# The four smallest experts moved last, and the final normalization started beside them, in a one-core mixture-of-experts layer

## The chip, the cores and the metric

The kernel runs on one core of one Trainium2 chip. The metric is device time in microseconds (us) for one execution, the median of the runs shown. Times inside a trace are counted from the first instruction of one profiled execution.

## The reference

One decoder layer on 1024 tokens of width 1024, in float32. The first sub-layer (token mixing, a projection, a layer norm) is not touched. The second is a mixture of experts: a router picks two of 32 experts for each token; an expert is a SwiGLU block with a 1024x1024 up matrix and a 512x1024 down matrix. The end of the layer is a second layer norm:

```
m = _hier_moe(h2, ...)          # for each token: sum over its 2 experts of weight * expert(h2)
x = _layernorm(ALPHA * x + (1.0 + g2) * m, ln2_g, ln2_b)
```

## The kernel before, in words

**What is computed where.** When the router is done, a table in DRAM, `xad` (1024 rows and 128 spare ones), holds `ALPHA * x` for each token. Each expert adds its weighted result to the rows of its tokens with an indirect DMA from POOL (`scatter`, line 1415). Every scatter adds into `xad`, so each waits until the one before has landed. At the very end (lines 1543 to 1603) `xad` is read back in eight tiles of 128 rows, each is normalized and stored to `out`.

**The order of the experts.** Experts 0 to 2 stand first. The other 29 are ranked by their number of tokens, and the table `place` (lines 841 to 844) says which rank is worked on at which of the 32 places in the order. Before the change large and small ones alternate to the end: places 25, 27, 29 and 31 hold the four smallest (ranks 28 to 31), place 26 one of five experts with room for two tiles of tokens, place 28 rank 11 and place 30 rank 15. An expert with at most 32 tokens runs a four-part form (`up_parts(4)`, `down_parts(4)`: matmuls with 32 columns of weights, 128\*32 in a row), up to 48 tokens (and up to 64) a two-part form (128\*64), a larger one the whole form (128\*128).

**One step of the loop** (lines 1480 to 1505), for place e: the first half of the up matrix (`up(e, range(4), ...)`), the transposes of the hidden tile of e-1, the second half of the up matrix, `hidden` (Silu on ScalarE, product on VectorE), the transposes of the tokens of e+1 with the gather for e+3 behind them, and then `last_of(e-1)`: the down matrix of e-1, `finish(e-1)` (VectorE scales the result, POOL scatters it).

**The weight stream.** Weights come as 384 loads of 512 KB on SP's queue, in the order of the list `SEQ` (lines 763 to 766): the eight up tiles of e, then the four down tiles of e-1. There are 38 slots. `release` (line 1460) hands a used slot back and issues the next load (`eload`, line 788). When all 384 are issued, two further releases fetch the norm's two vectors (`late_v`, line 1445: ln2_g and ln2_b, each broadcast to a 128x1024 tile, `l2`). Instructions of one queue are issued in program order, so a load that has to wait holds up every load behind it on SP.

**The end.** After `last_of(31)` every engine reads one number (`most`, line 1512) and jumps over a block for very large experts (`tc.If`, line 1513), which is not taken here. Then the eight reads of `xad`, and 59 steps of normalization, whose order is the string `TORDER` (one digit for a step of that tile) and whose engines are set by `TSTAT` (moments on VectorE or ScalarE) and `TMODE` (which engine does the multiplication by ln2_g, step `both(0)`, and the addition of ln2_b, step `both(1)`). In the first thirteen steps, 0010010210121, stand the moments of tiles 0 to 2, the roots of tiles 0 and 1, and as the thirteenth the `both(0)` of tile 1 on VectorE (line 1574), the first VectorE step that needs ln2_g.

Of the kernel before, what the change touches and what calls it, by code (L numbers as in the profile page):

```python
# [23 lines left out]
P = 128  # L24
# [7 lines left out]
FIXED = 3  # L32
SPREAD = 4
BIG = (3, 5, 12, 19, 26)
CO = (1, 2)
HL = 5
WK = (6,)
# [15 lines left out]
TSTAT = "VVVSVSVS"  # L53
TMODE = "pFBpFAFF"
TORDER = "00100102101213023231320425323423564546436567545653776777575"
BACC = dict(dynamic_dma_scratch_size=7168)
COLS = [slice(0, 512), slice(512, 1024)]

# [2 lines left out]
def tile_hybrid_moe_layer(  # L61
# [31 lines left out]
    def cst(shape, dt, name):  # L93
        return const.tile(shape, dt, name=name)
# [1173 lines left out]
    def reorder():  # L1268
# [19 lines left out]
    nmax = cst([P, 1], I32, "nmax")  # L1288
    places()
    for t in (*xg[2:], *eyo, yo2, act, *wr, *wr2):  # L1290
        G.memset(t, 0.0)
# [126 lines left out]
                             compute_op=OP.add)  # L1418

    def finish(e):  # L1420
        yo = eyo[e % 2]
        by_parts(N[e], lambda: result(yo, pd(e), wr[e % 2]), lambda m: result(yo, pd(e), wr[e % 2], m))
        by_size(rows_of(e), lambda rows: scatter(yo, tokp[:, 0, e:e + 1], rows))
# [50 lines left out]
    def last_of(e):  # L1474
# [2 lines left out]
        finish(e)  # L1477
        finish_second(e)

    for e in range(NE):  # L1480
# [62 lines left out]
    l2g, l2b = l2  # L1543
# [3 lines left out]
    st8 = p4.tile([P, 8, 2, 6], F32, name="st8")  # L1547
    mv8 = p4.tile([P, 8, 2], F32, name="mv8")

    def t_ops(tt):  # L1550
        r, mode = rt[tt], TMODE[tt]
        mu, sd = mv8[:, tt, 0:1], mv8[:, tt, 1:2]

        def moments():
            for n, sl in enumerate(COLS):
                V.bn_stats(st8[:, tt, n], r[:, sl])

        def root(scale=1.0):
            S.activation(sd, sd, AF.Sqrt, bias=eps, scale=scale)

        def shift():
            if TSTAT[tt] == "V":
                V.scalar_tensor_tensor(mu, mu, -1.0, sd, op0=OP.mult, op1=OP.mult)
            else:
                V.tensor_tensor(mu, mu, sd, op=OP.mult)

        def part(q, sl, fused, e):
            v = (l2g, l2b)[q]
            if not fused:
                e.tensor_tensor(r[:, sl], r[:, sl], v[:, sl], op=(OP.mult, OP.add)[q])  # L1570
            elif q:
                V.scalar_tensor_tensor(r[:, sl], r[:, sl], sd, v[:, sl], op0=OP.mult, op1=OP.add)  # L1572
            else:
                V.scalar_tensor_tensor(r[:, sl], r[:, sl], mu, v[:, sl],  # L1574
                                       op0=OP.subtract if TSTAT[tt] == "V" else OP.add, op1=OP.mult)

        def both(q):
            e = {"p": (G, G), "F": (V, V), "A": (G, V), "B": (V, G), "X": (V, V), "q": (G, G)}[mode][q]
            for sl in COLS if tt == 7 else [slice(0, D)]:
                part(q, sl, mode == "F", e)  # L1580
                if q and tt == 7:
                    nc.sync.dma_start(out[0, tt * P:(tt + 1) * P, sl], r[:, sl])
            if q and tt < 7:
                nc.sync.dma_start(out[0, tt * P:(tt + 1) * P, :], r)

        if TSTAT[tt] == "V":
            ops = [moments, lambda: V.bn_aggr(mv8[:, tt], st8[:, tt]), root]
        else:
            ops = [lambda: S.activation(eyo[0], r, AF.Copy, accum_out=mu),
                   lambda: V.tensor_scalar(mu, mu, -1.0 / D, None, op0=OP.mult),  # L1590
                   lambda: S.activation(eyo[0], r, AF.Square, bias=mu, accum_out=sd),
                   lambda: root(1.0 / D)]
        ops.append(lambda: V.reciprocal(sd, sd))
        if mode == "q":
            ops.append(lambda: V.tensor_scalar(r, r, mu, sd, op0=OP.subtract if TSTAT[tt] == "V" else OP.add,
                                               op1=OP.mult))
        elif mode != "F":
            ops += [shift, lambda: S.activation(r, r, AF.Identity, bias=mu, scale=sd)]
        return ops + [lambda: both(0), lambda: both(1)]

    t_all = [t_ops(tt) for tt in range(8)]
    for tt in TORDER:
        run(t_all[int(tt)], 1)


_INS = ['x', 'c', 'w_ada', 'b_ada', 'w_in', 'lb_logits', 'hg_norm_w', 'sg_ln_g', 'sg_ln_b', 'sg_w', 'sg_b',
# [20 lines left out]
```

## Time and profile before

| | us |
|---|---|
| three runs | 1179.14, 1181.39, 1178.46 |
| median | 1179.14 |
| profiled execution, own time | 1183.11 |
| profiled execution, span of its trace | 1181.4 |
| TensorE busy in the span | 1042.4 (88%) |
| VectorE, ScalarE, POOL busy | 553.6, 291.6, 359.6 |

The span runs from the first to the last instruction, and the execution's own time lies 1.7 us above it. Shares over the whole span mix stages with different limits; the change concerns the last 160 us, so the rows below are from there. A row of the timeline gives the start, the time, the engine, the line, the operation with what it writes and reads, the shape, how many instructions the row merges, and in brackets how long the engine sat idle before and what released it. "SPq" is SP's queue of DMA issues: its rows show the issue, not the transfer.

### The profile page before, as it was taken

The numbers are of one execution on the slowest core, as the hardware profiler recorded it, in microseconds if no ns is written. First come the engines' busy times: TensorE is split into PE (matmuls) and PEld (weight loads), VectorE is DVE, ScalarE is ACT, GpSimd is POOL, SyncE is SP. The second block draws the span as 40 slices with busy tenths as digits, with TensorE's granted clock in tenths as the row PEclk, the third lists the DMA queues.
The fourth block names the chain that finished last, engine by engine and source line by source line (L and its number), as shares of the span: only waits on it lengthen the run. The fifth ranks groups of instructions, "written<-read, shape, count | busy, mean of one in ns | idle before, by whom it ended". The sixth has DMA issues, their size and how long they took to land. (4 is left out here: it accounts for less than half of the span.)

```text
span 1181.4 us, 17353 instructions
## 1 busy us (share of the span) xinstructions
PE 1042.4 (88%) x5758; PEld 678.4 (57%) x5758; DVE 553.6 (47%) x1018; ACT 291.6 (25%) x440; POOL 359.6 (30%) x272
## 2 busy tenths in 40 slices
PE   4999999899999989998588899999998998799930
PEld 3778888788788767776333454445433553344400
DVE  6858975738664389999410211311221121211238
ACT  3363336642234442121200110101110110110113
POOL 2325643353121145552511211321141113211215
PEclk9899999999999998999799999999998998999975
DMA  9854454343211336316899979999999999999964
GB/s 278 241 164 146 143 178 144 124 157 130 89 54 54 143 143 220 120 72 248 303 393 383 351 254 371 363 386 390 371 379 395 393 371 372 394 398 384 378 247 187
DMA packets 121282, 304.55 MB, mean 258 GB/s; under 512 B 17840, under 2 KB 45144, under 8 KB 121132
## 3 DMA queue, kind: packets, MB, share of 16 engines
q1 hardware_dynamic: 111548, 275.53, 64.1%
q0 software_dynamic: 8368, 22.90, 7.2%
q10 hardware_dynamic: 1216, 4.21, 0.9%
q8 instruction: 83, 1.36, 0.5%
q14 instruction: 67, 0.55, 0.1%
HBM read 281.09 MB, written 22.88 MB: 257 GB/s over the span
## 5 line engine op out<-in xcount | busy, mean ns | idle before, releaser
L1395 DVE TENSOR_TENSOR act<-up,act 128x512 f32<-128x512 f32 x32 | 22.1, 692 | 311.6 <-ACT act L1394 234.1
L1416 POOL DMA_INDIRECT xad<-yo,tokp x36 | 52.8, 1466 | 228.4 <-DVE yo L1412 141.5
L1412 DVE SCALAR_TENSOR_TENSOR yo<-dn,wr,g2p 32x256 f32<-32x256 f32 (+2 forms) x94 | 52.1, 563 | 127.4 <-PE ov L1348 49.3
L1401 ACT ACTIVATE eh<-tp 128x512 f32<-128x512 f32 x36 | 21.1, 596 | 311.3 <-PE tp L1400 268.5
L1207 POOL DMA_INDIRECT KS<-h2d,tokp x32 | 30.5, 954 | 191.5 <-PE tp L1311 182.8
L622 PE MATMUL acc<-whi,hTh 128*128 128x512 f32 x192 | 83.0, 433 | 0.0
L166 ACT ACTIVATE whi<-wr 128x1024 fp32r<-128x1024 f32 (+1 forms) x44 | 44.9, 1021 | 128.3 <-PE acc L624 67.0
L624 PE MATMUL acc<-whi,hTl 128*128 128x512 f32 x192 | 75.9, 396 | 0.0
L623 PE MATMUL acc<-wlo,hTh 128*128 128x512 f32 x192 | 75.4, 392 | 0.0
L167 POOL TENSOR_TENSOR wlo<-wr,whi 128x1024 fp32r<-128x1024 f32 (+1 forms) x15 | 35.8, 2384 | 119.4 <-ACT whi L166 112.6
L1343 PE MATMUL up<-pring,ext 128*32 128x256 f32 (+1 forms) x564 | 53.4, 439 | 13.5 <-DMA pring<-in_w_up 10.7
L302 PEld LDWEIGHTS sm<-QP,KS 128*128 128x128 f32 x448 | 58.2, 192 | 7.3 <-issue 3.2
L618 PE MATMUL acc<-hTh,whi 128*128 128x512 f32 x144 | 59.2, 411 | 0.0
L302 PE MATMUL sm<-QP,KS 128*128 128x64 f32 x448 | 56.1, 269 | 2.6 <-DVE KS L315 1.6
L620 PE MATMUL acc<-hTh,wlo 128*128 128x512 f32 x144 | 56.9, 395 | 0.5 <-POOL wlo L167 0.2
L619 PE MATMUL acc<-hTl,whi 128*128 128x512 f32 x144 | 56.6, 393 | 0.0
L1336 PE MATMUL up<-pring,ext 128*128 128x512 f32 x128 | 56.6, 592 | 0.0
L877 PE MATMUL pa<-wh,yl 128*128 128x512 f32 (+1 forms) x128 | 51.8, 405 | 4.7 <-DVE yl L861 4.7
L876 PE MATMUL pa<-wl,yh 128*128 128x512 f32 (+1 forms) x128 | 51.6, 403 | 4.7 <-DVE wl L1048 4.7
L1394 ACT ACTIVATE act<-up 128x512 f32<-128x512 f32 x32 | 19.1, 597 | 144.4 <-PE ov L1336 52.3
L875 PE MATMUL pa<-wh,yh 128*128 128x512 f32 (+1 forms) x128 | 53.6, 419 | 1.3 <-ACT wh L1047 0.9
L443 POOL TENSOR_TENSOR vec<-vec,y1a 128x1024 f32<-128x1024 f32 x14 | 35.8, 2560 | 55.2 <-ACT y1a L442 55.2
(493 smaller groups left out, 2225.2 us busy)
## 6 DMA issues: line engine op xcount, KB each, us to landing
pring<-in_w_up SPq DMA_DIRECT2D x112, 512.0 KB
pring<-in_w_down SPq DMA_DIRECT2D x58, 512.0 KB
wr<-in_w_in SPq DMA_DIRECT2D x44, 512.0 KB
ring<-in_w_up SPq DMA_DIRECT2D x42, 512.0 KB
y1a<-in_w_ada SPq DMA_DIRECT2D x32, 512.0 KB
ring<-in_w_down SPq DMA_DIRECT2D x18, 512.0 KB
y0a<-in_w_up SPq DMA_DIRECT2D x16, 512.0 KB
y0b<-in_w_up SPq DMA_DIRECT2D x16, 512.0 KB
```

What stands on the lines that cost most here:

```text
L302: PE.matmul(p[:, hd], chd(KS)[:, c4, hd], chd(QP)[:, c4, hd].rearrange("p (b two i) -> p b two i", two=2, i=h)[:, :, 1, :], start=True, st ...
L618: PE.matmul(a[i], hi[:, j, sl], hTh[k], start=st, stop=False)
L619: PE.matmul(a[i], hi[:, j, sl], hTl[k], start=False, stop=False)
L620: PE.matmul(a[i], lo[:, j, sl], hTh[k], start=False, stop=sp)
L622: PE.matmul(a[i], hTh[k][:, sl], hi[:, j], start=st, stop=False)
L623: PE.matmul(a[i], hTh[k][:, sl], lo[:, j], start=False, stop=False)
L624: PE.matmul(a[i], hTl[k][:, sl], hi[:, j], start=False, stop=sp)
L875: PE.matmul(p, yh[:, k], wh[k][:, sl], start=k == 0, stop=False)
L1336: PE.matmul(p[:, h], x[:, k], gate_up(w[k], 2, h), start=k == 0, stop=k == 7)
L1343: PE.matmul(o[j * r:(j + 1) * r], x[:, k, 0:r], gate_up(w[k], m, j), start=k == 0, stop=k == 7)
L1412: V.scalar_tensor_tensor(yo[rows, n * c:(n + 1) * c], src, w[rows], g2p[rows, n * c:(n + 1) * c], op0=OP.mult, op1=OP.mult)
L1416: G.indirect_dma_start(out=xad, out_offset=bass.IndirectOffsetOnAxis(ap=tcol[rows], axis=0), in_=yo[rows], in_offset=None, bounds_check=T ...
```

## The change

Four parts. **(a) The order:** ranks 15 and 11 move from places 30 and 28 to places 25 and 27, and the four smallest ranks take places 28 to 31. **(b) No scatter for the last four:** if each of them has at most 32 tokens (and nothing needs the block for very large experts), their results are written to rows 0, 32, 64 and 96 of one tile, `yo2`. The old rows of their tokens are gathered from `xad` into a tile `base`; at the end a matmul with a 0/1 matrix (`same`: which rows belong to the same token) sums the results, the sum is added to `base`, that tile is normalized, and its rows are scattered to `out`. Otherwise the old way is taken. **(c) The reads:** the eight tiles of `xad` are read at the end of step 28, behind `last_of(27)`, into eight slots whose releases issue no load (`KEPT`). **(d) The normalization:** of the same 59 steps 16 stand ahead of `hidden(31)`, 5 ahead of `last_of(30)`, 6 ahead of `last_of(31)`'s transposes, 3 beside the sum of the last tile, the other 29 behind it. The eight tiles are stored whole, the late tokens' rows in them without their last experts, and these rows are written over by the scatter at the end. The bodies of `late_loads`, of `t_ops` and of `finish_any` are those of before.

```diff
+LATE0 = 28
+NL = (16, 5, 6, 3)
...
+    for o, n, base in ((25, 1, 15), (27, 1, 11), (LATE0, 4, LATE0)):
+        G.iota(place[:, o:o + n], pattern=[[1, n]], base=base, channel_multiplier=0, **imp)
...
+        V.tensor_reduce(slowi, nhp[:, LATE0:NE], axis=AX.X, op=OP.max)
+        V.tensor_scalar(slowi, slowi, 9.0, None, op0=OP.is_gt)
+        V.tensor_tensor(slowi, slowi, nmax, op=OP.max)
+        for i in range(4):
+            V.tensor_copy(tokl[32 * i:32 * (i + 1)], tokp[0:32, 0, LATE0 + i:LATE0 + i + 1])
+        V.tensor_copy(tokf, tokl)
...
     def finish(e):
+        if e < LATE0:
+            finish_any(e)
+            return
+        r = 32 * (e - LATE0)
+        with tc.If(slow > 0) as large:
+            finish_any(e)
+        with large.Else():
+            for q in range(4):
+                sl = slice(q * 256, (q + 1) * 256)
+                V.scalar_tensor_tensor(yo2[r:r + 32, sl], pd(e)[32 * q:32 * (q + 1), 0, 0:256], wr[e % 2][0:32],
+                                       g2p[0:32, sl], op0=OP.mult, op1=OP.mult)
...
+    KEPT = [(LATE0, k) for k in range(4, 8)] + [(LATE0 - 1, k) for k in range(8, 12)]
+
     def release(e, ks):
         for k in ks:
             unused.append(RAW[place_of[e, k]])
-            eload()
+            if (e, k) not in KEPT:
+                eload()
...
+    def late_start():
+        rt.extend(unused.popleft() for _ in range(8))
+        late_loads()
+        G.indirect_dma_start(out=base, out_offset=None, in_=xad,
+                             in_offset=bass.IndirectOffsetOnAxis(ap=tokl, axis=0), bounds_check=T + P - 1,
+                             oob_is_err=False)
+        V.tensor_scalar(act2[:, 0:P], ones, tokf, None, op0=OP.mult)
+        p = tp()
+        PE.matmul(p[:, 0], act2[:, 0:P], ident, start=True, stop=True)
+        V.tensor_scalar(same, p[:, 0], tokf, None, op0=OP.is_equal)
+
+    def late_sum():
+        for n in range(2):
+            PE.matmul(pup[:, n], same, yo2[:, COLS[n]], start=True, stop=True)
+
+    def late_norm():
+        for n, sl in enumerate(COLS):
+            V.tensor_tensor(base[:, sl], pup[:, n], base[:, sl], op=OP.add)
+            V.bn_stats(st8[:, 8, n], base[:, sl])
+        mu, sd = mv8[:, 8, 0:1], mv8[:, 8, 1:2]
+        V.bn_aggr(mv8[:, 8], st8[:, 8])
+        S.activation(sd, sd, AF.Sqrt, bias=eps, scale=1.0)
+        V.reciprocal(sd, sd)
+        V.scalar_tensor_tensor(base, base, mu, l2[0], op0=OP.subtract, op1=OP.mult)
+        V.scalar_tensor_tensor(base, base, sd, l2[1], op0=OP.mult, op1=OP.add)
+
+    def late_store():
+        G.indirect_dma_start(out=out[0], out_offset=bass.IndirectOffsetOnAxis(ap=tokl, axis=0), in_=base,
+                             in_offset=None, bounds_check=T - 1, oob_is_err=False)
...
     for e in range(NE):
+        if e == LATE0:
+            slow = count(slowi, 0, [mybir.EngineType.DVE, mybir.EngineType.Pool], 1)
         up(e, range(4), weights_of(e, range(4)))
...
         up(e, range(4, 8), weights_of(e, range(4, 8)))
         release(e, range(4, 8))
+        if e == NE - 1:
+            norms(NL[0])
         hidden(act, pup)
         hidden_second(e)
         turn_first(e + 1)
+        if e == NE - 1:
+            norms(NL[1])
         if e:
             last_of(e - 1)
         if e + 1 < NE:
             turn_second(e + 1)
+        if e == LATE0:
+            late_start()
+    norms(NL[2])
     turn_hidden(act, eh)
     turn_hidden_second(NE - 1)
     last_of(NE - 1)
-    most = count(nmax, 0, None, 1)
-    with tc.If(most > 0):
+    slow_all = count(slowi, 0, None, 1)
+    with tc.If(slow_all > 0) as large:
...
-    rt = [unused.popleft() for _ in range(8)]
-    for tt in range(8):
-        nc.sync.dma_start(rt[tt], xad[tt * P:(tt + 1) * P, :])
...
+        late_loads()
+        rest_of = [t_ops(tt) for tt in range(8)]
+        for tt in TORDER:
+            run(rest_of[int(tt)], 1)
+    with large.Else():
+        late_sum()
+        norms(NL[3])
+        late_norm()
+        norms()
+        late_store()
```

## Rows read from the trace of the kernel before

**Rows 1.** Busy time by stretch: PE, PEld, DVE, ACT, POOL (instructions), PEclk, DMA share, GB/s

```profile
1020.00:1080.00 60.00, 57.80 (x282) 27.72 (x283) 11.18 (x20) 6.07 (x11) 8.15 (x8) 1.00 1.03 399
1080.00:1134.00 54.00, 50.41 (x351) 22.16 (x349) 11.80 (x20) 6.97 (x12) 13.45 (x11) 0.97 1.00 368
...
1160.30:1177.70 17.40, 0.00 (x0) 0.00 (x0) 16.75 (x21) 6.71 (x12) 12.14 (x4) 0.50 0.40 159
```

**Rows 2.** Timeline of SP's queue near the end

```profile
1109.31 1.61 SPq L103 DMA_DIRECT2D ring<-in_w_up  x2
...
1123.27 0.33 SPq L103 DMA_DIRECT2D gs<-in_w_down  x1
1124.48 0.34 SPq L1446 DMA_DIRECT2D vn<-in_ln_g  x1
...
1143.32 0.81 SPq L1546 DMA_DIRECT2D y0a<-xad  x2
```

**Rows 3.** Timeline of TensorE in the expert stage

```profile
952.34 7.03 PE L1336 MATMUL up<-pring,ext 128*128 128x512 f32 x16
...
1006.83 4.45 PE L1355 MATMUL dn<-pring,eh 128*64 128x512 f32 x16
...
1018.60 0.64 PE L1343 MATMUL up<-ring,ext 128*32 128x256 f32 x8 [0.82 <-DMA ring<-in_w_up]
...
1058.14 1.91 PE L1343 MATMUL up<-pring,ext 128*32 128x256 f32 x32
...
1115.97 1.93 PE L1355 MATMUL dn<-pring,eh 128*32 128x256 f32 x32
...
1134.06 0.64 PE L1355 MATMUL ov<-gs,eh 128*32 128x256 f32 x8 [0.56 <-DMA gs<-in_w_down]
```

**Rows 4.** Chain that ended last: three scatters, from issue to landing (start, us)

```profile
1079.48 9.70 DMA xad<-yo,tokp
...
1100.27 6.42 DMA xad<-yo,tokp
...
1109.05 10.22 DMA xad<-yo,tokp
```

**Rows 5.** Timeline of VectorE, ScalarE, POOL and SP behind the last weights

```profile
1092.54 0.69 DVE L1395 TENSOR_TENSOR act<-up,act 128x512 f32<-128x512 f32 x1 [12.02 <-ACT act L1394]
...
1130.79 0.60 ACT L1401 ACTIVATE eh<-tp 128x512 f32<-128x512 f32 x1 [6.30 <-PE tp L1400]
...
1134.18 1.28 ACT L1559 ACT_TABLE_LOAD   x1 [2.79 <-ACTq L1513]
1134.77 1.96 DVE L1412 SCALAR_TENSOR_TENSOR yo<-ov,wr,g2p 32x256 f32<-32x256 f32 x4 [3.02 <-PE ov L1355]
1138.19 1.31 POOL L1416 DMA_INDIRECT xad<-yo,tokp  x1 [4.75 <-DMA xad<-yo,tokp]
...
1146.43 1.29 DVE L1556 BATCH_NORM_STATS2 st<-y0a 128x6 f32<-128x512 f32 x2 [9.71 <-DMA y0a<-xad]
...
1149.59 1.23 ACT L1598 ACTIVATE y0a<-y0a,mv 128x1024 f32<-128x1024 f32 x1
...
1150.90 5.63 POOL L1570 TENSOR_TENSOR y0a<-y0a,vn 128x1024 f32<-128x1024 f32 x2 [11.40 <-ACT y0a L1598]
...
1151.46 2.86 DVE L1574 SCALAR_TENSOR_TENSOR y0a<-y0a,mv,vn 128x1024 f32<-128x1024 f32 x1
...
1154.38 3.24 DVE L1572 SCALAR_TENSOR_TENSOR y0a<-y0a,mv,vn 128x1024 f32<-128x1024 f32 x1
...
1170.50 1.28 DVE L1572 SCALAR_TENSOR_TENSOR uu<-uu,mv,vn 128x1024 f32<-128x1024 f32 x1
...
1177.68 0.33 SPq L1584 DMA_DIRECT2D out<-y1a  x1
```

**Rows 6.** Line 1513, the jump over the block for very large experts, on VectorE's queue

```profile
L1513 DVEq EVENT_SEMAPHORE  x2: 21/21/21, 1138.6 to 1138.7; - x2
```

**Rows 7.** One of the small VectorE steps that follow the router's table

```profile
L1286 DVE TENSOR_REDUCE nmax<-nb x1: 186/186/186, 585.2 to 585.2; 128x1 int32<-128x32 int32 x1
```

More of the change, by code (lines that the diff above doesn't have):

```diff
@@ L1286, in reorder @@
         V.tensor_reduce(nmax, nb, axis=AX.X, op=OP.max)
+        V.tensor_reduce(slowi, nhp[:, LATE0:NE], axis=AX.X, op=OP.max)
[4 more added lines that the diff above has]
+        V.tensor_copy(tokf, tokl)
     nmax = cst([P, 1], I32, "nmax")
+    slowi = p4.tile([P, 1], I32, name="slow")
+    tokl = p4.tile([P, 1], I32, name="tokl")
+    tokf = p4.tile([P, 1], F32, name="tokf")
     places()
@@ L1420, in finish, with finish_any @@
     def finish(e):
+        if e < LATE0:
[9 more added lines that the diff above has]
+                                       g2p[0:32, sl], op0=OP.mult, op1=OP.mult)
+    def finish_any(e):
         yo = eyo[e % 2]
@@ L1478, in last_of, with late_loads @@
         finish_second(e)
+    st8 = p4.tile([P, 9, 2, 6], F32, name="st8")
+    mv8 = p4.tile([P, 9, 2], F32, name="mv8")
+    same = p4.tile([P, P], F32, name="same")
+    rt, junk = [], []
+    base = xg[2]
+    def late_loads():
+        for tt in range(8):
+            nc.sync.dma_start(rt[tt], xad[tt * P:(tt + 1) * P, :])
+    def late_start():
[8 more added lines that the diff above has]
+        V.tensor_scalar(same, p[:, 0], tokf, None, op0=OP.is_equal)
@@ new lines, in late_store, with t_ops, moments, root @@
+    def late_store():
+        G.indirect_dma_start(out=out[0], out_offset=bass.IndirectOffsetOnAxis(ap=tokl, axis=0), in_=base,
+                             in_offset=None, bounds_check=T - 1, oob_is_err=False)
+    def t_ops(tt):
+        r, mode = rt[tt], TMODE[tt]
+        mu, sd = mv8[:, tt, 0:1], mv8[:, tt, 1:2]
+        def moments():
+            for n, sl in enumerate(COLS):
+                V.bn_stats(st8[:, tt, n], r[:, sl])
+        def root(scale=1.0):
+            S.activation(sd, sd, AF.Sqrt, bias=eps, scale=scale)
+        def shift():
+            if TSTAT[tt] == "V":
+                V.scalar_tensor_tensor(mu, mu, -1.0, sd, op0=OP.mult, op1=OP.mult)
+            else:
+                V.tensor_tensor(mu, mu, sd, op=OP.mult)
+        def part(q, sl, fused, e):
+            v = (l2[0], l2[1])[q]
+            if not fused:
+                e.tensor_tensor(r[:, sl], r[:, sl], v[:, sl], op=(OP.mult, OP.add)[q])
+            elif q:
+                V.scalar_tensor_tensor(r[:, sl], r[:, sl], sd, v[:, sl], op0=OP.mult, op1=OP.add)
+            else:
+                V.scalar_tensor_tensor(r[:, sl], r[:, sl], mu, v[:, sl],
+                                       op0=OP.subtract if TSTAT[tt] == "V" else OP.add, op1=OP.mult)
+        def both(q):
+            e = {"p": (G, G), "F": (V, V), "A": (G, V), "B": (V, G), "X": (V, V), "q": (G, G)}[mode][q]
+            for sl in COLS if tt == 7 else [slice(0, D)]:
+                part(q, sl, mode == "F", e)
+                if q and tt == 7:
+                    nc.sync.dma_start(out[0, tt * P:(tt + 1) * P, sl], r[:, sl])
+            if q and tt < 7:
+                nc.sync.dma_start(out[0, tt * P:(tt + 1) * P, :], r)
+        if TSTAT[tt] == "V":
+            ops = [moments, lambda: V.bn_aggr(mv8[:, tt], st8[:, tt]), root]
+        else:
+            ops = [lambda: S.activation(junk[0], r, AF.Copy, accum_out=mu),
+                   lambda: V.tensor_scalar(mu, mu, -1.0 / D, None, op0=OP.mult),
+                   lambda: S.activation(junk[0], r, AF.Square, bias=mu, accum_out=sd),
+                   lambda: root(1.0 / D)]
+        ops.append(lambda: V.reciprocal(sd, sd))
+        if mode == "q":
+            ops.append(lambda: V.tensor_scalar(r, r, mu, sd, op0=OP.subtract if TSTAT[tt] == "V" else OP.add,
+                                               op1=OP.mult))
+        elif mode != "F":
+            ops += [shift, lambda: S.activation(r, r, AF.Identity, bias=mu, scale=sd)]
+        return ops + [lambda: both(0), lambda: both(1)]
@@ L1480, in tile_hybrid_moe_layer, with norms @@
+    todo_norms = []
+    def norms(n=99):
+        if not todo_norms:
+            junk.append(eyo[0] if not unused else unused[0])
+            t_all = [t_ops(tt) for tt in range(8)]
+            todo_norms.extend(t_all[int(tt)] for tt in TORDER)
+            todo_norms.append([])
+        for _ in range(min(n, len(todo_norms) - 1)):
+            run(todo_norms.pop(0), 1)
     for e in range(NE):
+        if e == LATE0:
+            slow = count(slowi, 0, [mybir.EngineType.DVE, mybir.EngineType.Pool], 1)
@@ L1540, in tile_hybrid_moe_layer @@
                     scatter(eyo[0], icol[:, 0:1], slice(0, P))
-    l2g, l2b = l2
-    rt = [unused.popleft() for _ in range(8)]
-    for tt in range(8):
-        nc.sync.dma_start(rt[tt], xad[tt * P:(tt + 1) * P, :])
[L1547 to L1599, printed above, removed]
@@ L1601, in tile_hybrid_moe_layer @@
-    t_all = [t_ops(tt) for tt in range(8)]
-    for tt in TORDER:
-        run(t_all[int(tt)], 1)
+        late_loads()
[8 more added lines that the diff above has]
+        late_store()
 _INS = ['x', 'c', 'w_ada', 'b_ada', 'w_in', 'lb_logits', 'hg_norm_w', 'sg_ln_g', 'sg_ln_b', 'sg_w', 'sg_b',
```

## The prediction

> **What bounds the kernel now.** I read the table of stretches first. Up to 1134 the DMA engines are busy all the time (share 1.00 to 1.03 at 368 to 399 GB/s), TensorE nearly so; in the last stretch VectorE works 16.75 of 17.4 us and POOL 12.1, DMA only 0.40 [rows 1]. So there are two stages with different limits: a weight stream bound by DMA, then a tail bound by VectorE and POOL. SP's queue shows where one ends: the last weight load is issued at 1123.27, the norm's vectors directly behind it, the first read of the rows at 1143.32 [rows 2]. TensorE takes the last weights as they land, at 1134.06 [rows 3], 10.8 us after the issue. The chain of waits then goes through scatters, 6.4 to 10.2 us each from issue to landing [rows 4]. The tail: the last scatter starts at 1138.19, first moments at 1146.43, first pass with ln2_g at 1150.90 (POOL) and 1151.46 (VectorE), last store issued at 1177.68 [rows 5], end at 1181.4. From 1150.90 to the end are 30.5 us: 26.8 of passes and 3.7 for the last store.
>
> The profiled execution's own time is 1183.1, 1.7 above its span and 4 above the median of 1179.1; I work in span and carry the difference over to the median.
>
> **The reads in the stream.** Eight reads of 512 KB are put among the loads, ahead of the last ten weights: eight of the 38 slots are kept back, so of the 384 loads the first 374, up to the sixth up tile of place 31, are issued before them. These eight transfers are moved, not saved, and DMA has nothing to spare there. At 399 to 368 GB/s [rows 1] one takes 1.31 to 1.42 us, eight 10.5 to 11.4. The decisive point is behind them: the two releases that fetch ln2_g and ln2_b are now the last two down tiles of place 28, so the vectors again come behind the last weight, and no multiplication by ln2_g can start earlier. Call T the moment when ln2_g has landed.
>
> **When SP may issue the reads.** They need every scatter up to place 27. The new order puts a whole-form expert at place 27 and a two-part one at 25. Up of 27: 2 x (7.03 - 1.91) = 10.2 us more; down of 25: 4.45 - 1.93 = 2.5 more [rows 3]. The up of 25 I cost at nothing, because TensorE waits there for each load (0.82 us before one [rows 3]); without that cover it would be 2 x 2.5. So the work behind place 26 starts 12.7 us later. Its first scatter, at 1079.48, moves to 1092.2; place 27's was issued 20.8 us behind that, 1100.27 [rows 4], so 1113.0 now; with its rows in whole form it lands like the one at 1109.05, 10.2 us later: 1123.2. SP comes to the reads about when it issued the seventh up tile of place 31, at 1109.31 [rows 2], and stands there for some 14 us, with the ten weights and the vectors queued behind it. The loads in flight last 10.8 us, to about 1119 or 1120: the DMA engines run dry for 4 to 6 us. TensorE, which waits for the seventh up tile, has nothing else.
>
> **T.** Reads issued at 1123.2; the first lands 3.1 us later (1143.32 to 1146.43 [rows 2, 5]), 1126.3; ln2_g is the nineteenth transfer, 18 x 1.37 = 24.7 behind: **T = 1151**. Low end, no dry time: 1134.1 + 9 x 1.31 = 1146. High end, with the gather of `base` (512 KB more) and the slow pace: 1126.3 + 19 x 1.42 = 1153, and 1155 for a scatter 2 us slower. So the vectors arrive when they were first used before, 1150.90. Nothing that needs them is early.
>
> **What is done before T.** Of 59 steps the first twelve on VectorE and ScalarE. The thirteenth, `both(0)` of tile 1, stops VectorE until T, and queued behind it are the product of `hidden(31)`, `finish(30)`, and through them the transposes, down and `finish(31)` on TensorE and ScalarE. POOL stops likewise at tile 0; its weight gathers for places 29 to 31 stand behind the gather of `base` and so behind the same scatter, but are done long before T.
>
> **What is behind T on VectorE.** The old 26.8 us of passes, and new among them: the product 0.69; `finish(30)` and `finish(31)` 1.96 each; between these the way of the last expert over the other engines: an Identity pass 1.23 and a sum of about the same, the copy to `eh` 0.60, four-part down 1.93, about 5.0, in which one tile's moments (1.29) and trifles of 0.2 fit, 3.5 left; the branch: VectorE's queue goes on at 1138.7, 2.0 after its last work ended at 1136.7; the late tile: two additions from PSUM, 0.69 each like the product, moments 1.29, aggregate, root and reciprocal some 0.6, two passes [rows 5, 6]. The two passes are 1.28 each alone, 2.9 to 3.2 beside a POOL pass (POOL's two took 5.63 in the same time [rows 5]); three POOL passes are waiting by then, so I take 2.9 each, 5.8. Sum 0.69 + 3.9 + 3.5 + 2.0 + 3.3 + 5.8 = 19.2. Off go the moments and roots finished early, 1 us at most behind 1150.90, and part of the stretch of passes beside POOL: two were 1.6 and 2.0 longer than alone, and POOL now runs some of its six while VectorE reads PSUM or waits. I take 5 for that (bounds 0 and 9). 26.8 + 19.2 - 1 - 5 = 40.
>
> The Trainium skill (SBUF — State Buffer, "SBUF: two separate sides") says that VectorE and POOL share a port pair as an exclusive lock, taken for a whole instruction, by VectorE operations with two SBUF inputs against POOL operations that read SBUF. The stretched passes above agree. By that rule the operations that read PSUM, the finishes and the additions, are not stretched, and the relief would stand nearer to 9 than to 0, the end some 3 us earlier.
>
> **The end.** After the last pass its store needs 3.7 us as before. The late tile's rows are written over rows of the stores, so the scatter to `out` has to wait for all of them, and POOL issues it last. The nearest row is the last scatter, 1138.19 to 1143.32, 5.1 us [rows 2, 5]; it may be 3 without the addition. Together 1151 + 40 + 3.7 + 5.1 = 1199.8 against 1181.4: 18.4 us longer. **1179.1 + 18.4 = 1197.5 us.**
>
> **Small edits.** Three more iotas and eight small steps at the table, each like the 0.186 us of [rows 7], about 2 us at 585 us, where the stream has not yet formed; I cost them at nothing, because the loads of the next experts, all issued ahead, set the pace; 2 us if not. `same` needs TensorE once and two VectorE steps in step 28, under the loads' shade. ScalarE changes its table to Sqrt and back around the last Silu: two loads more of 1.28 [rows 5], one before T, one beside VectorE's passes. The four scatters saved take little off DMA; what they gave the end, the 9.7 us in which VectorE waited for the rows [rows 5], is the gain of the change, and it is spent on the later stream.
>
> **The rivals.**
> *Room in the stream (faster).* If DMA could carry the reads beside the weights, the weights and vectors would still be there at 1136. Then 27 steps are done before the last down, and behind 1134.7 come finish 2.0, branch 2.0, three steps 1.7, the late tile 9.1, the other 29 steps about 14, and 8.8: 1172, that is 1170 for the median. The point is whether eight transfers fit without moving the last weight; a share of 1.00 speaks against it, only the change of pace between 368 and 399 GB/s for it. Chance 0.05.
> *Vectors in time.* If VectorE is not stopped at ln2_g (the vectors ahead of the last weights), only the stream is longer: last weight at 1149.6, then the same 38 us: 1187.5, 6 slower; without dry time 1182, no change. The release count speaks against it. Chance 0.08, half of it within 0.3%.
> *No dry time.* The scatter lands before the loads in flight are used up: T = 1146, 1193 for the median. Inside the main case.
> *The change does not do what it says.* If one of the four had over 32 tokens, everything is read and normalized again behind the stream: above 1205. The places 25, 27, 29 and 31 show the 32-column form in every row of theirs [rows 3], so 0.02.
>
> **How the numbers follow.** Main case 0.83: T from 1146 to 1155 and the chain from 35 to 44 us, 1188 to 1206. With the rivals on its lower side the range is 1184 to 1206. A measurement of this kernel tells 0.3% (3.5 us) from no change; faster by more 0.06, within 0.05, slower 0.89.
>
> **What would show it.** Right: SP's first read of `xad` issued near 1123, 10 to 14 us behind the load before it, and waiting for the scatter; a dip of the DMA share around 1120; the last weight landing near 1149; VectorE idle in front of `both(0)` of tile 1 until ln2_g has landed, then busy to the end; a scatter to `out` issued 3 to 4 us after the last store. Wrong: the last weight before 1142, ln2_g landing ahead of it, a chain behind T under 33 us, or no wait before the last scatter.

## The result, and the profile after

The changed kernel takes 1200.35 us (median of four runs, 1200.28 to 1202.10) against 1180.27 us of the kernel before on the same chip. These medians lie 20.1 us apart; the ratio on record, by which the text goes from here on, is 1.0179, 95% interval 1.0160 to 1.0199, or 21 us more. The prediction was 1197.5 us, range 1184 to 1206. The profiled execution took 1202.1 us, its span is 1200.3.

Profiled executions reach the expert stage at slightly different times, so ends are also compared from a landmark ahead of it, the step that finds the largest expert [rows 7]. It is the following row of the changed kernel (a row of one line's instructions: shortest, median and longest in ns, first and last start):

```profile
L1290 DVE TENSOR_REDUCE nmax<-nb x1: 186/186/186, 583.8 to 583.8; 128x1 int32<-128x32 int32 x1
```

From there to the end are 616.5 us, against 1181.4 - 585.2 = 596.2 before: 20.3 us. All of the loss lies behind the router.

SP's queue, timeline, of the kernel after, and under it the longest wait of that queue (total, times, longest):

```profile
1097.16 8.60 SPq L105 DMA_DIRECT2D pring<-in_w_up  x6
1119.19 4.46 SPq L1522 DMA_DIRECT2D ring<-xad  x6
...
1137.43 1.60 SPq L105 DMA_DIRECT2D y1a<-in_w_down  x2
1139.94 0.34 SPq L1473 DMA_DIRECT2D uu<-in_ln_g  x1
...
1154.70 27.31 SPq L1588 DMA_DIRECT2D out<-ring  x5
...
1189.62 0.33 SPq L1588 DMA_DIRECT2D out<-ring  x1
```

```profile
SPq L1522 <- DMA xad<-yo,tokp: 13.3, 1, 13.3
```

The reads stand in front of the last ten weights, and SP stands 13.3 us at the first of them, for a scatter. Which scatter, POOL's timeline shows:

```profile
1090.36 1.61 POOL L1430 DMA_INDIRECT xad<-yo,tokp  x1 [14.54 <-DVE yo L1426]
1101.08 1.46 POOL L1430 DMA_INDIRECT xad<-yo,tokp  x1 [9.11 <-DMA xad<-yo,tokp]
...
1110.18 1.62 POOL L1430 DMA_INDIRECT xad<-yo,tokp  x1 [5.02 <-DMA xad<-yo,tokp]
1119.33 1.03 POOL L1527 DMA_INDIRECT xg<-xad,tokl  x1 [7.53 <-DMA xad<-yo,tokp]
...
1150.22 6.65 POOL L1574 TENSOR_TENSOR ring<-ring,uu 128x1024 f32<-128x1024 f32 x2 [19.20 <-DMA uu<-in_ln_g]
...
1193.78 1.02 POOL L1551 DMA_INDIRECT out<-xg,tokl  x1 [7.86 <-POOLq L1657]
```

Place 27's scatter is issued at 1110.18, as soon as the one before it has landed, and has landed itself when SP goes on at 1119.19, 9 us later. The table of stretches (columns as in [rows 1]) shows what DMA did meanwhile:

```profile
1080.00:1110.00 30.00, 28.09 (x194) 13.55 (x196) 6.27 (x11) 3.25 (x6) 5.08 (x4) 0.94 1.03 378
1110.00:1117.00 7.00, 6.55 (x106) 3.78 (x106) 2.90 (x6) 1.14 (x3) 1.62 (x1) 1.00 0.78 208
1117.00:1122.00 5.00, 4.95 (x74) 3.22 (x72) 1.29 (x2) 0.78 (x2) 2.06 (x3) 1.00 0.45 122
1122.00:1150.00 28.00, 7.85 (x64) 1.83 (x64) 6.26 (x16) 6.76 (x10) 1.97 (x2) 0.59 0.97 375
...
1173.00:1189.60 16.60, 0.00 (x0) 0.00 (x0) 16.18 (x21) 5.72 (x11) 8.94 (x3) 0.50 0.29 116
```

Where all 54 us from 1080 to 1134 were at a share of 1.00 before [rows 1], the share falls to 0.78 and 0.45 between 1110 and 1122, and all the other engines do little in the 28 us behind that. TensorE gets its next weights at 1137.36; in the kernel before it had its last at 1134.06 [rows 3]:

```profile
1137.36 1.08 PE L1357 MATMUL up<-wsg,ext 128*32 128x256 f32 x8 [13.87 <-DMA wsg<-in_w_up]
```

VectorE's timeline is the rest of the story:

```profile
1150.10 1.28 DVE L1578 SCALAR_TENSOR_TENSOR ring<-ring,mv,uu 128x1024 f32<-128x1024 f32 x1 [15.94 <-DMA uu<-in_ln_g]
...
1154.70 1.97 DVE L1444 SCALAR_TENSOR_TENSOR yo<-dn,wr,g2p 32x256 f32<-32x256 f32 x4
...
1163.44 1.99 DVE L1444 SCALAR_TENSOR_TENSOR yo<-ov,wr,g2p 32x256 f32<-32x256 f32 x4 [5.30 <-PE ov L1369]
1166.79 1.23 DVE L1574 TENSOR_TENSOR ring<-ring,uu 128x1024 f32<-128x1024 f32 x1 [1.36 <-issue]
...
1173.28 3.24 DVE L1548 SCALAR_TENSOR_TENSOR xg<-xg,mv,uu 128x1024 f32<-128x1024 f32 x1
...
1188.38 1.21 DVE L1574 TENSOR_TENSOR ring<-ring,uu 128x1024 f32<-128x1024 f32 x1
```

Its first pass with ln2_g waits 15.94 us and starts at 1150.10, as good as where the kernel before had it, 1151.46 (POOL 1150.90) [rows 5]. Everything that the change added then stands behind it: both late finishes, a hole of 5.30 us between them, the late tile, and the same passes as before. The wait of 9.71 us for the rows [rows 5] is gone, and a wait of 15.94 us for the vector stands in its place.

### The profile page after: what moved, and what is told of

Its sections match the earlier page's. It is cut to its first block, busy times and chain, and to the rows that moved or that the text cites. A ratio compares the mean times of both kernels' runs of the same rounds, so it can differ in the third digit from the quotient of the medians.

```text
span 1200.3 us, 17393 instructions
## 1 busy us (share of the span) xinstructions
PE 1049.4 (87%) x5764; PEld 680.2 (57%) x5764; DVE 556.6 (46%) x1036; ACT 294.8 (25%) x443; POOL 356.6 (30%) x273
## 5 line engine op out<-in xcount | busy, mean ns | idle before, releaser
L1430 POOL DMA_INDIRECT xad<-yo,tokp x32 | 47.5, 1486 | 205.4 <-DVE yo L1426 124.2
L1426 DVE SCALAR_TENSOR_TENSOR yo<-dn,wr,g2p 32x256 f32<-32x256 f32 (+2 forms) x82 | 46.4, 576 | 125.6 <-PE ov L1362 50.5
L1350 PE MATMUL up<-pring,ext 128*128 128x512 f32 x144 | 63.7, 593 | 0.0
L1357 PE MATMUL up<-pring,ext 128*32 128x256 f32 (+1 forms) x552 | 49.4, 430 | 11.4 <-DMA pring<-in_w_up 9.4
```

Source lines behind the costliest of these rows:

```text
L1350: PE.matmul(p[:, h], x[:, k], gate_up(w[k], 2, h), start=k == 0, stop=k == 7)
L1357: PE.matmul(o[j * r:(j + 1) * r], x[:, k, 0:r], gate_up(w[k], m, j), start=k == 0, stop=k == 7)
```

## The experiments

Theory: the time went into three things, one behind the other. (1) SP stands at the reads with weights and vectors behind it; (2) the two vectors come behind the last weight and stop VectorE; (3) sixteen steps of the norm were put ahead of the last expert's product, so a stopped step stops the expert. Rival: the order of the experts itself costs it, or the eight transfers as such.

| run | median us | ratio to before | 95% interval | end behind the landmark, us |
|---|---|---|---|---|
| before | 1179.14 | 1 | | 596.2 |
| after | 1200.35 | 1.0179 | 1.0160 to 1.0199 | 616.5 |
| 1 order alone | 1181.57 | 1.0018 | 1.0005 to 1.0031 | 596.3 |
| 2 vectors first | 1193.55 | 1.0118 | 1.0090 to 1.0145 | 605.6 |
| 3 reads on ScalarE's queue | 1199.18 | 1.0172 | 1.0154 to 1.0189 | 613.5 |
| 4 steps later | 1190.79 | 1.0104 | 1.0085 to 1.0124 | 605.3 |
| 5 reads last | 1194.18 | 1.0138 | 1.0121 to 1.0155 | 608.1 |
| 6 reads on POOL's queue | 1190.68 | 1.0096 | 1.0080 to 1.0113 | 604.4 |
| 7 vectors first, reads on POOL's queue, steps earlier, 9 of them last | 1188.61 | 1.0095 | 1.0058 to 1.0131 | 599.9 |
| 8 as 7, no step last | 1178.46 | 0.9996 | 0.9984 to 1.0008 | 593.4 |
| 9 as 8, 35 steps behind the expert | 1189.85 | 1.0085 | 1.0072 to 1.0098 | 601.7 |
| 10 as 8, 15 steps behind it | 1183.84 | 1.0035 | 1.0023 to 1.0047 | 600.9 |
| 11 as 8, 4 steps behind it | 1181.02 | 1.0013 | 1.0004 to 1.0023 | 593.7 |
| 12 as 8, 7 steps behind it | 1182.54 | 1.0024 | 1.0012 to 1.0036 | 595.2 |

The runs were made on several chips, each beside the kernel before on the same chip (medians there from 1178.87 to 1180.27), and the ratios are those on record; a median of the table divided by its own kernel before differs from its ratio by up to 0.0016. The last column is of one execution each. That of the kernel before was 4 us above its median, so the column is read for where the time lies and the ratios for how much.

**1. The order alone.** The kernel before with the three lines that change the order, and nothing else of the change:

```diff
         G.iota(spread[:, :, j], pattern=[[step, 4]], base=base, channel_multiplier=0, **imp)
+    for o, n, base in ((25, 1, 15), (27, 1, 11), (28, 4, 28)):
+        G.iota(place[:, o:o + n], pattern=[[1, n]], base=base, channel_multiplier=0, **imp)
```

> The kernel before with the new order of the experts alone (three more iotas; the end as before). Theory (the stop at ln2_g and the longer stream make the loss): the stream of weights is bound by DMA, so its end stays at 1134 and the time within 0.3% of the kernel before, 1177 to 1184. Rival (the order: large experts late in the table, small ones last, keep TensorE busy past the stream, or their later scatters hold the reads): 5 to 15 us slower, the last weight used well after 1134.

1181.57 us, 0.18% slower, so the theory held. The last weight is used at 1127.10, 545.2 us behind the landmark (1127.10 - 581.9), against 548.9 before (1134.06 [rows 3]): TensorE is not busy past the stream. In POOL's timeline the last scatters now queue up behind each other, where before only the last one waited for its forerunner:

```profile
1123.98 1.35 POOL L1418 DMA_INDIRECT xad<-yo,tokp  x1 [5.30 <-DMA xad<-yo,tokp]
...
1130.61 1.34 POOL L1418 DMA_INDIRECT xad<-yo,tokp  x1 [3.95 <-DMA xad<-yo,tokp]
1135.58 1.30 POOL L1418 DMA_INDIRECT xad<-yo,tokp  x1 [3.64 <-DMA xad<-yo,tokp]
```

Even so the last one is issued 553.7 us behind the landmark, against 553.0 before. The order costs 2 of the 21 us by the ratio, and nothing that the two profiled executions could tell (596.3 against 596.2). The rival that blames it is out.

**2. The vectors first.** Two more slots are kept back, and the two vectors are issued ahead of the reads:

```diff
-    KEPT = [(LATE0, k) for k in range(4, 8)] + ...
+    KEPT = [(LATE0, k) for k in range(2, 8)] + ...
     def late_start():
+        for _ in range(2):
+            late.popleft()(unused.popleft())
```

> The changed kernel with ln2_g and ln2_b loaded ahead of the eight reads (two more slots kept), nothing else. Theory (the stop at ln2_g): VectorE no longer stands idle from 1134 to 1150; the 27 steps ahead of the last down are done while weights land; the last weight lands near 1151 and what follows the last expert's result takes the 36.9 us it takes in the changed kernel (1163.4 to 1200.3): span 1188 to 1191, ratio to before 1.005 to 1.010. Rival (the tail is the passes' own length on VectorE and POOL, wherever they start): span 1197 to 1201, no gain over the changed kernel.

1193.55 us: of the 21 us, 0.61% or 7 us are gone, a little less than expected (1.0118 where 1.005 to 1.010 was). SP still stands at the reads, 13.7 us, and the weights still come late, but VectorE no longer waits for a vector. The last finish comes at 1154.54 us, 568.6 behind the landmark, against 579.6 after (1163.44 - 583.8).

**3, 5 and 6. Where the reads are issued.** Three ways to keep SP's queue from standing. In run 3 the reads go to ScalarE's queue, two steps later, so that SP could go on:

```diff
-    def late_loads():
+    def late_loads(q=nc.sync):
         for tt in range(8):
-            nc.sync.dma_start(rt[tt], xad[tt * P:(tt + 1) * P, :])
+            q.dma_start(rt[tt], xad[tt * P:(tt + 1) * P, :])
...
         rt.extend(unused.popleft() for _ in range(8))
-        late_loads()
...
         turn_first(e + 1)
+        if e == LATE0 + 2:
+            late_loads(nc.scalar)
```

> The changed kernel with the eight reads issued from ScalarE's queue behind the product of place 30, so that SP doesn't stand in front of them and the last ten weights and the vectors flow on. Theory (part of the loss is the dry time of DMA while SP waits for a scatter, 1110 to 1122, worth 4 us of transfers): vectors land near 1146, span 1195 to 1197. Rival (no loss from the wait, since the loads in flight cover it): span 1199 to 1201. If the vectors now even pass the reads, they land as early as 1138 and the span falls to 1190 or below.

1199.18 us, as good as nothing. SP's longest wait in this run, and ScalarE's queue:

```profile
SPq L105 <- DMA ring<-xad: 17.6, 1, 17.6
```

```profile
1119.88 7.11 ACTq L1522 DMA_DIRECT2D ring<-xad  x6
1128.34 1.45 ACTq L1522 DMA_DIRECT2D more<-xad  x2
1129.89 0.60 ACT L1415 ACTIVATE eh<-tp 128x512 f32<-128x512 f32 x1 [15.48 <-DMA ring<-xad]
```

SP stands even longer, now at a weight load (line 105) that waits for a read of the other queue, though it writes another slot. In the compiled program the transfers of both queues take turns on eight completion semaphores, and each waits for the eighth before it; the loads behind the reads thus wait for the reads. The trace names them: 100 and 102 to 108 for SP's and ScalarE's transfers, 111 to 118 for POOL's, and the load that stands uses 103, as the fifth read did. And ScalarE's own work stands 15.5 us behind its issues. My expectation had not seen this. The run says nothing for or against (1); it moved the wait.

In run 5 the reads stay on SP's queue, but at the end of step 29, behind all weights and both vectors:

```diff
         rt.extend(unused.popleft() for _ in range(8))
-        late_loads()
...
             late_start()
+        if e == LATE0 + 1:
+            late_loads()
```

> The changed kernel with the eight reads issued on SP's queue at the end of step 29, behind the last ten weights and the two vectors. Theory (what counts is when ln2_g lands; reads ahead of the weights delay it and the wait for the scatter adds dry time): weights and vectors land some 18 us earlier, the rows 1.3 us apart behind them; the first pass with ln2_g starts about 12 us earlier than in the changed kernel, everything behind it takes as long as there: 9 to 12 us less than the changed kernel, 1.007 to 1.011 of the kernel before. Rival (the reads ahead of the weights do hide the rows, and late rows cost what early vectors give): within 3 us of the changed kernel.

1194.18 us: 0.41% or 5 us gained, where 9 to 12 were expected. SP does not stand any more, but the reads are now what is late (SP, then VectorE):

```profile
1119.70 0.34 SPq L1473 DMA_DIRECT2D uu<-in_ln_g  x1
...
1122.60 7.76 SPq L1522 DMA_DIRECT2D ring<-xad  x6
```

```profile
1133.90 1.29 DVE L1559 BATCH_NORM_STATS2 st<-ring 128x6 f32<-128x512 f32 x2 [5.91 <-DMA ring<-xad]
```

In run 6 the reads go to POOL's queue (`late_loads` takes a queue, as in run 3), ahead of the gather of `base`, with the weight gather for place 29 moved ahead of them:

```diff
         rt.extend(unused.popleft() for _ in range(8))
-        late_loads()
+        gather_weight(LATE0 + 1, 0)
+        late_loads(G)
...
-        gather_weight(e, 0)
+        if e != LATE0 + 1:
+            gather_weight(e, 0)
```

> The changed kernel with the eight reads issued from POOL's queue, ahead of the gather of base, and the weight gather of place 29 ahead of them. In the run with ScalarE's queue the loads on SP still stood for 17.6 us behind the reads, since both queues take turns at the same eight completion semaphores; POOL's transfers have others. Theory (dry time of DMA while SP waits is part of the loss): the DMA share between 1110 and 1122 stays above 0.9, the last weight and ln2_g land 4 to 6 us earlier, 3 to 6 us less than the changed kernel. Rival (the loads in flight cover the wait): no more than 1 us less.

1190.68 us: 0.83%, nearly 10 us gained, more than the 3 to 6 expected. POOL waits for the scatter, SP does not, and the table of stretches has no dip:

```profile
1119.72 3.26 POOL L1522 DMA_DIRECT2D ring<-xad  x6 [7.92 <-DMA xad<-yo,tokp]
```

```profile
1110.00:1117.00 7.00, 4.84 (x72) 2.83 (x68) 1.87 (x5) 1.62 (x3) 1.50 (x2) 1.00 1.05 339
1117.00:1122.00 5.00, 3.23 (x56) 1.99 (x52) 1.68 (x4) 0.10 (x1) 2.28 (x5) 1.00 1.02 405
...
1122.00:1136.00 14.00, 6.58 (x83) 3.43 (x72) 5.70 (x15) 4.76 (x8) 4.13 (x6) 0.87 1.03 407
```

```profile
1140.71 1.28 DVE L1579 SCALAR_TENSOR_TENSOR ring<-ring,mv,uu 128x1024 f32<-128x1024 f32 x1 [6.38 <-DMA uu<-in_ln_g]
```

ln2_g has landed at 1140.71, 554.8 behind the landmark, against 566.3 after. By bytes: after moved 7 x 208 + 5 x 122 + 28 x 375 = 12,570 KB from 1110 to 1150; at the rates of this run the same bytes take 7 + 5 us and (12,570 - 2,373 - 2,025) / 407 = 20.1 more, 8 us less. The trace agrees: the last of the reads, weights, vectors and the gather of `base` lands 567.5 us behind the landmark after (ln2_b, at 1151.3) and 559.4 in run 6 (the gather, at 1145.3). So SP's wait cost the stream 8 us. Another 1.6 us of run 6's gain lie at the very end and have another cause (under "The end" below).

**4. The steps later.** No step of the norm beyond the twelfth ahead of the last expert's finish:

```diff
-NL = (16, 5, 6, 3)
+NL = (12, 0, 0, 18)
```

> The changed kernel with NL = (12, 0, 0, 18): the first pass that needs ln2_g and all behind it moved past the last expert, the late tile still behind 30 steps. Theory (the last expert stands behind the stop, and its product, two finishes, the way over the other engines and the branch are paid after ln2_g has landed): the last result is ready near 1152 instead of 1165, and 7 to 9 us are gained: span 1191 to 1194. Rival (the work on VectorE is only reordered, the sum of passes sets the end): span 1198 to 1201.

1190.79 us, 0.75% or 9 us gained. VectorE and POOL:

```profile
1144.97 1.99 DVE L1444 SCALAR_TENSOR_TENSOR yo<-ov,wr,g2p 32x256 f32<-32x256 f32 x4 [3.46 <-PE ov L1369]
1148.39 2.88 DVE L1578 SCALAR_TENSOR_TENSOR ring<-ring,mv,uu 128x1024 f32<-128x1024 f32 x1 [1.43 <-issue]
```

```profile
1145.42 4.77 POOL L1574 TENSOR_TENSOR ring<-ring,uu 128x1024 f32<-128x1024 f32 x2 [20.10 <-DMA uu<-in_ln_g]
```

The last finish now starts just ahead of ln2_g's landing (1145.42) instead of 13.3 us behind it. From that landing to the end are 1187.1 - 1145.4 = 41.7 us, against 50.2 after: 8.5 us. That the landing itself came 2.7 us earlier behind the landmark than after (563.6 against 566.3) is not the run's doing, since the reads ahead of it were issued as much earlier (532.7 against 535.4).

**7 and 8. Three moves together.** The vectors first (as in 2), the reads on POOL's queue (as in 6), and, since vectors and rows are there early, the opposite of run 4: more steps ahead of the last expert instead of fewer, 26, 14, 10 and 0 in place of 16, 5, 6 and 3 in run 7, 30, 14, 15 and 0 in run 8. What is left of the 59 stands behind the late tile.

> Three parts together: vectors ahead of the rows, reads on POOL's queue, and NL = (26, 14, 10, 0), so that 50 of the 59 steps stand ahead of the last expert's transposes and nine behind the late tile. Theory (the loss is order, not work: with the vectors there, VectorE, ScalarE and POOL have 20 us beside the last ten weights): behind the last weight stand the last expert's result, the branch, the sum, the late tile's 8 us, some 5 us of passes and the two waits of 4 and 6.5 us: 8 to 14 us faster than the kernel before, 0.988 to 0.993. Rival (VectorE's and POOL's passes hold up the last expert's product and copies on their engines, or DMA's 4 MB of stores hold up the last weights): not faster than the kernel before.

Run 7 missed, and its rival held: 1188.61 us, 1.0095. The late tile was finished, and nine steps and their stores stood behind it; the last store was issued at 1176.17, and only behind that the final scatter, at 1180.68.

> As the run before with NL = (30, 14, 15, 0): all 59 steps ahead of the last expert's transposes. Theory: if the steps are done before the last weight lands, another 4 to 6 us less than with nine behind; if they are not, ScalarE's copy for the last expert waits for them and it is the same or up to 4 us slower than that run. Rival as there.

Run 8 ends level with the kernel before, 0.9996: 1.0% less than run 7, where 4 to 6 us less, the same or more were expected. VectorE, ScalarE and POOL of run 8:

```profile
1139.46 2.29 DVE L1572 TENSOR_TENSOR mv<-mv 128x1 f32<-128x1 f32 x1
...
1158.15 1.21 DVE L1577 TENSOR_TENSOR ring<-ring,pring 128x1024 f32<-128x1024 f32 x1
1159.39 1.99 DVE L1444 SCALAR_TENSOR_TENSOR yo<-ov,wr,g2p 32x256 f32<-32x256 f32 x4
1163.52 0.69 DVE L1544 TENSOR_TENSOR xg<-up,xg 128x512 f32<-128x512 f32 x1 [2.14 <-PE up L1540]
...
1168.30 1.28 DVE L1551 SCALAR_TENSOR_TENSOR xg<-xg,mv,pring 128x1024 f32<-128x1024 f32 x1
```

```profile
1153.73 0.58 ACT L1415 ACTIVATE eh<-tp 128x512 f32<-128x512 f32 x1
```

```profile
1170.00 1.02 POOL L1554 DMA_INDIRECT out<-xg,tokl  x1 [14.31 <-POOLq L1661]
```

No store is left behind the late tile, so the final scatter follows its last pass at once, and there is no idle time before the last finish: between the copy to `eh` (1153.73) and that finish (1159.39) VectorE has steps to do. The eight reads stand among the weights here too, so the transfers as such do not make the 21 us.

**9 to 12. The last expert sooner.** In run 8 the last expert's finish stands behind every step, though its weights are there long before. So runs 9 to 12 keep some steps back, behind that finish and ahead of the late tile: `NL = (0, 12, 12, 35)`, `(0, 24, 20, 15)`, `(30, 14, 11, 4)` and `(30, 14, 8, 7)`.

> The run before it (all three moves, 30, 14 and 15 steps of the norm in the last three places, none behind) ended level with the kernel before the change, with the last expert's finish at 1159.4 us behind every step of the norm. Here the same three moves, but no step in the last expert but two's place of the thirty: 0, 12, 12 and, behind the last expert's finish and ahead of the late tile, 35. Theory: the steps only stood ahead of the last expert on ScalarE and VectorE, whose weights were there long before; with the expert let through, its finish moves to about 1145, its scatter lands beside the remaining steps, and the end comes 3 to 6 us earlier: 0.993 to 0.997 of the kernel before. Rival: the sum of VectorE's work sets the end wherever the expert stands, and the order only exchanges what is last: 0.998 to 1.002.

> As the run beside it, with the steps spread 0, 24, 20 and 15 instead, so that more of them fill the time until the last expert's weights have landed and fewer stand behind it. Theory: 0.993 to 0.997 of the kernel before, level with the run beside it within 2 us, since both have the expert's finish ahead of the last steps. Rival, that the sum of VectorE's work sets the end: 0.998 to 1.002 for both.

> All three moves, steps 30, 14, 11 and 4 in place of 30, 14, 15 and 0. In the run with none behind, VectorE is nearly dense from 1124 to 1168 us, with 2.14 us idle between the last expert's finish and the late tile. Theory: order is worth something only where it fills idle time, so four steps behind the finish fill these 2 us and the end comes 1 to 2 us earlier: 0.997 to 0.999 of the kernel before. Rival, from the two runs with 35 and 15 behind, which were slower: any step kept behind the last expert's finish costs, since VectorE then waits ahead of it: 1.001 to 1.004.

> As the run beside it with 30, 14, 8 and 7. Theory: 0.996 to 1.000, the 2 us between finish and late tile filled and up to 2 us of idle time ahead of the finish in their place. Rival: 1.002 to 1.005, on the way to the 1.0035 of fifteen behind.

The first two missed both theory and rival: 1.0085 and 1.0035, slower, and 6 us apart. So the order is neither free nor a gain. For the last two the rival held: 1.0013 and 1.0024, slower by 2 and 3 us, the first just clear of nothing (from 1.0004). VectorE of run 9, and of run 11:

```profile
1142.00 1.97 DVE L1444 SCALAR_TENSOR_TENSOR yo<-dn,wr,g2p 32x256 f32<-32x256 f32 x4 [10.78 <-DMA wr<-wd,aidp]
```

```profile
1160.31 1.99 DVE L1444 SCALAR_TENSOR_TENSOR yo<-ov,wr,g2p 32x256 f32<-32x256 f32 x4 [4.05 <-PE ov L1369]
```

In run 9 VectorE has nothing to do for 10.78 us, until POOL's gather of routing weights, itself behind the gather of `base`, has landed (8.53 in run 10). Its last finish does come 9.7 us sooner behind the landmark than run 8's (568.3 against 578.0), and the end 8.3 us later. In run 11 it is idle for 4.05 us between the copy to `eh` and the finish (5.52 in run 12), because the steps that filled this hole in run 8 are the ones that were put behind; the copy itself came only 1.5 us sooner (570.9 against 572.3 us behind the landmark): a step on ScalarE ahead of it waits 3.81 us for VectorE in both runs. A step put behind the expert opens a hole ahead of it and is still to be done. No version that I tried beats the kernel before.

## Why the prediction was right

**Reads issued, 1123.2 forecast: 1119.2.** The mechanism held: SP waits 13.3 us (some 14 forecast) for place 27's scatter. The scatter landed in 9.0 us instead of 10.2 and was issued at 1110.2 instead of 1113.0, of which 1.4 us is the earlier landmark. The step behind it, that the new order delays place 26's first scatter to 1092.2, came out at 1090.36.

**Dry time, 4 to 6 us forecast: the stream lost about 8.** The share that the DMA engines lack, 0.22 of 7 us and 0.55 of 5 us, is 4.3 us, as forecast. But they moved less in the share that they had, and run 6 puts the whole loss at 8 us: this term was too small. Eighteen transfers at 1.37 us behind the first were to bring ln2_g 27.8 us after the issue of the reads; it took 30.9 (1119.19 to 1150.10). TensorE's row shows where: `wsg`, the ninth transfer, is there at 1137.36, 18.2 us after the issue, where 3.1 + 8 x 1.37 = 14.1 were expected; the ten from there to ln2_g take 12.7, 1.27 each. In the trace the first read lands 4.6 us after its issue (1123.80) instead of 3.1, and the second 3.6 us behind it (1127.44), with the gather of `base` landing between them (1127.20): 512 KB that the forecast had only in its high end.

**T, 1151 forecast: 1150.1.** Two errors, 4 us early and 3 us late, nearly cancel. That T came out within 1 us is luck; that the vectors come behind the last weight (which landed at 1148.8, 1149 forecast) and hold VectorE is not.

**The chain behind T, 40 us forecast: 39.5** (1150.1 to 1189.6). Here too errors cancel. The way between the two finishes took 6.8 us with 5.3 idle (5.0 and 3.5 forecast). The forecast took 1.93 us for the last expert's down from a row at full clock; it took 3.64:

```profile
1159.73 1.93 PE L1369 MATMUL ov<-y0b,eh 128*32 128x256 f32 x16 [6.46 <-ACT eh L1415]
1161.44 1.93 PE L1369 MATMUL ov<-y1a,eh 128*32 128x256 f32 x16
```

Sixteen matmuls took as long as 32 did in the kernel before [rows 3]: the granted clock was 0.50 here, against 0.97 in the stretch of that row [rows 1]. Those 1.7 us are what the hole has over its forecast. The branch took 1.4 (2.0), and the late tile's two passes 1.27 and 3.24 (5.8 together); the price of the stretch, 2.9 for each, was right for one of two. The relief of the old passes, 5 forecast, was 6.2: VectorE's passes of the eight tiles, with one small step that waited among them, sum to 22.6 us before and 16.4 after. The Trainium skill's rule on the shared port pair (SBUF — State Buffer, "SBUF: two separate sides") put the end 3 us earlier; the operations that it exempts were indeed not stretched (the finish at 1154.70 took 1.97 beside a POOL pass that began at 1150.22). The relief lies between the forecast's and the one by that rule, and the longer hole took back what it had over the 5.

**The end, 3.7 and 5.1 us forecast: 4.2 and 6.5.** The last store was issued at 1189.62, the scatter to `out` at 1193.78, the end is 1200.3. The second term was mis-sized, and not by the scatter: in the trace it lands at 1197.03, 3.25 us after its issue, and the last scatter of the kernel before, with addition, took as long (1138.19 to 1141.45). The forecast's 5.1 ended at SP's next issue instead. What it left out is POOL's last instruction, a drain, which runs from 1194.88 to 1199.49, 4.6 us. It took that in every run with the reads on SP's or ScalarE's queue and about 3.0 in every run with the reads on POOL's, where the end came 4.8 to 5.3 us behind the scatter's issue. Why is open.

**Small edits and order, nothing forecast.** Run 1 prices the order, with its three iotas, at 2 us (0.6 to 3.7 by its interval); the forecast missed it. The eight small steps at the table no run prices alone.

Together: 18.4 us forecast; measured 20.3 by the profiles and 21 by the ratio.

**The rivals.** Run 2 makes "vectors in time" true, and it is 14 us slower than before, not 6. The rival's own tail was right, 37.6 us from the last finish to the end (1154.54 to 1191.6 is 37.1), but it let that finish follow the last weight at once, at 1150.3; it was 4 us later. The last expert's copy to `eh` stood behind two steps on ScalarE until 1150.8, and its down took 3.6 us, again at half the clock. "Room in the stream" is not borne out: with no stop of SP (run 6) the DMA share stays at 1.02 to 1.05, and the last vector lands 1143.3 - 585.9 = 557.4 us behind the landmark. In run 1, without the reads, the last weight was used at 545.2, two more transfers at 1.27 make 547.7: the reads (seven of the eight had landed by then) cost some 10 us of stream, near the 10.5 to 11.4 forecast for eight. They were moved, not hidden.

**What the runs add.** The forecast named step (3), that the expert stands behind a stopped step, and had its price in the chain: the product, the first finish and the hole, 0.69 + 1.96 + 3.5 = 6.2 us. Measured these are 0.69 + 1.97 + 5.30 = 8.0, and run 4, which takes them out from behind T, has 8.5 less there. Runs 2, 4 and 6 each undo one of the three for 7, 9 and 10 us. Run 8 undoes (1) and (2) and, with the vectors there, puts more steps ahead of the expert instead of fewer; against the changed kernel it gives 0.0183 of 1179.5, 21.6 us, the whole loss. How much of that belongs to the two moves and how much to the other split of the steps stays open: the moves of runs 2 and 6 with the old split, or with that of run 4, were not run. Nor was another choice of the steps' engines, with which run 8 might beat the kernel before.

## What to carry to other kernels

Before a transfer is put early into a queue, look at what it waits for and what is queued behind it: a read that waits 13 us takes every load behind it along, and the stream has to fill up again afterwards. Work that is started early is only early if its last operand is, so follow every operand (here two vectors at the end of the list) to its place in the queue. In these runs steps put ahead of a critical hop between engines were worth having as long as they filled its idle time: kept back, they left a hole (runs 9 to 12), and a stopped one stopped the hop (after, against run 4). And a price taken from a row holds only at that row's clock: the same down took 1.9 us in the busy stream and 3.6 behind it.

## What the runs showed of the hardware

- A transfer on ScalarE's queue held SP's queue up for 17.6 us (run 3), by the completion semaphores that the program's two queues share (100 and 102 to 108 in its trace); on POOL's queue the same transfers held up nobody on SP (run 6).
- A VectorE step on 128x1 took 2.29 us beside a POOL pass (run 8, 1139.46) and 0.15 elsewhere (1167.94 after). It was lengthened by 2.1 us, passes of 128x1024 by 1.6 and 2.0 [rows 5]: in these rows the addition does not grow with the operation.
- TensorE's granted clock was 0.59 in the stretch from 1122 to 1150, in which the engine waited 13.87 us for a weight, and 0.50, the lower of its levels (1.2 GHz), from 1159 to 1163.5. Eight matmuls took 1.08 us instead of 0.64 [rows 3]. For weights that came 1.27 us apart that cost next to nothing, for the last expert's down 1.7 us on the path to the end.
- A scatter to `out` landed 3.2 to 3.3 us after its issue in all runs, and so did the last scatter with addition in the kernel before. The end came 6.5 us behind that issue where POOL's last instruction, a drain, took 4.6, and 4.8 to 5.3 where it took about 3.0.
- The landmark ahead of the experts moved between 581.4 and 586.0 us over the profiled executions, more than most differences in this study; only ends counted from it, or ratios of many runs, could tell them apart.
